# A fused softmax maximum: the pass that adds bias or mask writes the negated, scaled row maximum

## The chip, the cores and the metric

The kernel runs on one core of a Trainium2 chip. The metric is the device time of one launch in microseconds (us), the median over runs of the kernel. Engines are named PE (TensorE, matmuls; PEld its weight loads), DVE (VectorE), ACT (ScalarE), POOL (GpSimd) and SP (SyncE, which issues the DMAs).

## The reference, cut to what matters

The program is a transformer stack on 512 tokens of width 1024 in fp32: four layers of a first block (MLA, sliding-window attention with sinks, attention with a forget gate ("fox"), MLA again), then a second block with four mixers, two of them attentions, a feed-forward part and a gated addition. Every attention is a softmax over rows of scores:

```python
s = einsum(q, k) * scale                      # MLA, fox, second block
s = s + c_q[:, None] - cum_t[None, :]         # fox only: forget gate
s = where(k_pos <= q_pos, s, -1e30)           # causal mask, or a window in the sliding-window layer
p = softmax(s, axis=-1)
o = einsum(p, v)
# the sliding-window layer has a sink per head:
m = maximum(max(s, axis=-1), sink)
p = exp(s - m)
p = p / (sum(p, axis=-1) + exp(sink - m))
```

A number that is constant along a row of `s` (such as `c_q`) changes no softmax.

## The kernel before, in words

There are 72 heads in all: 16 in each of the four layers of the first block and 8 in the second block. Each head goes once through `attend` (L395 to L461). A head has 512 queries, which are four blocks of 128 (i = 0 to 3, one query on each partition). In the causal attentions block i has 128, 256, 384 or 512 keys, in the sliding-window layer 128, 256, 256 and 256.

For a head, in program order: PE writes the score products of a block to PSUM (tiles ps_s; L159 to L161 in the MLA layers, L240 and L241 elsewhere). DVE reads them once (L408, in the trace CUSTOM_DVE_ANT_0 with a DVE_READ_ACCUMULATOR2_ANT behind it): it adds the bias or mask, writes the sum to the tile p in SBUF and leaves the maximum of each row in a column of the small tile st (128 x 4 for the four blocks). Small instructions on st then make the bias of the exponential: one on DVE for the MLA and second-block heads (L417), two for fox (L414 and L415, which add and take away the row's own forget value `cq`), two for the sliding window (L419 and L420, which also take in the sink) and there one more on ACT (L421, the sink's own exponential). ACT takes the exponential of the four blocks in place (L424) and leaves their row sums in st. DVE inverts these (L427) and multiplies p by them (L432). PE transposes p in pieces of 128 x 128 (L448), ACT and DVE split the transposed tile into a high and a low part (L186, pth; L187, ptl), PE multiplies by the values (L457, tile ps_o), and ACT and DVE add the two halves up (L467, L468). In the second block a step of a top-k search on DVE (`tick`, L930 and L931) stands between the row maxima and the small instructions.

Beside a head, PE has the projections of the next pair of heads and gates. Their weights come by DMA, ACT rounds them to a high part (L140), and POOL takes the low part (L141).

The order on each engine is not the program order. The tile framework is opened with `schedule_with_timeline_sim=True`: it places the instructions of all engines by a simulation of their times, within the data dependences, so an instruction that is taken away can move others on every engine. Each engine then works its own list in order.

Of the kernel before, what the change touches and what calls it, by code (L numbers as in the profile page):

```python
# [11 lines left out]
AF = mybir.ActivationFunctionType  # L12
ALU = mybir.AluOpType
PSUM = bass.MemoryType.PSUM

P, S, D, T = 128, 512, 1024, 4
# [74 lines left out]
class Kern:  # L91
# [300 lines left out]
        return nxt  # L392


    def attend(s, s_mm, k0s, bias, scale, v, sink=None, shift=None):  # L395


        nc = s.nc
        w = [(i + 1 - k0s[i]) * P for i in range(T)]
        off = [sum(w[:i]) for i in range(T)]  # L400
        sc = s.t("p", [P, sum(w)])
        st = s.t("st", [P, 8, T])
        for grp in (([[3], [2, 0], [1]] if w[3] == 512 else [[0, 2], [1, 3]])):
            ps = s.p("s")
            c = 0
            for i in grp:
                s_mm(ps[:, c:c + w[i]], i, k0s[i])
                nc.vector.tensor_tensor_reduce(out=sc[:, off[i]:off[i] + w[i]], in0=ps[:, c:c + w[i]], in1=bias(i),  # L408
                                               op0=ALU.add, op1=ALU.max, scale=1.0, scalar=-3e38,
                                               accum_out=st[:, 0, i:i + 1])  # L410
                c += w[i]
        s.tick(4)
        if shift is not None:
            nc.vector.scalar_tensor_tensor(st[:, 0], st[:, 0], scale, shift, op0=ALU.mult, op1=ALU.add)  # L414
            nc.vector.tensor_sub(st[:, 1], shift, st[:, 0])  # L415
        elif sink is None:
            nc.vector.tensor_scalar_mul(st[:, 1], st[:, 0], -scale)  # L417
        else:
            nc.vector.tensor_scalar(st[:, 0], st[:, 0], scale, sink, op0=ALU.mult, op1=ALU.max)  # L419
            nc.vector.tensor_scalar_mul(st[:, 1], st[:, 0], -1.0)  # L420
            nc.scalar.activation(st[:, 4], st[:, 0], AF.Exp, bias=sink, scale=-1.0)  # L421
        for i in range(T):
            a = sc[:, off[i]:off[i] + w[i]]
            nc.scalar.activation(a, a, AF.Exp, bias=st[:, 1, i:i + 1], scale=scale, accum_out=st[:, 2, i:i + 1])  # L424
        if sink is not None:
            nc.vector.tensor_add(st[:, 2], st[:, 2], st[:, 4])
        nc.vector.reciprocal(st[:, 3], st[:, 2])  # L427
        for i in range(T):
            a = sc[:, off[i]:off[i] + w[i]]
            how = ("vvvv" if "cq" in s.phase_tags else "aavp")[i]  # L430
            if how == "v":
                nc.vector.tensor_scalar_mul(a, a, st[:, 3, i:i + 1])  # L432
            elif how == "a":
                nc.scalar.mul(a, a, st[:, 3, i:i + 1])
            else:
                nc.gpsimd.tensor_mul(a, a, st[:, 3, i:i + 1].to_broadcast([P, w[i]]))
        s.tick(2)
        o = s.p("o")
        first = True
        for grp in (([[0], [1, 3], [2]] if w[3] == 512 else [[0, 1], [2, 3]])):  # L440
            ps = s.p("t")
            n, js = 0, []
            for j in grp:
                qs = [i for i in range(j, T) if k0s[i] <= j]
                js.append((j, n, len(qs) * P))
                for i in qs:
                    c = off[i] + (j - k0s[i]) * P
                    nc.tensor.transpose(ps[:, n:n + P], sc[:, c:c + P], s.ident)  # L448
                    n += P
            ph = s.t("pth", [P, S], R)  # L450
            pl = s.t("ptl", [P, S], R)
            s.split(ps[:, :n], ph[:, :n], pl[:, :n])
            s.tick(2)
            for j, c, m in js:
                vj = v(j)
                for k, pp in enumerate((ph, pl)):
                    s.last_mm = nc.tensor.matmul(o[:, j * P:j * P + m], vj, pp[:, c:c + m], start=first,  # L457
                                                 stop=k == 1 and grp[-1] == max(2, grp[-1]) and j == grp[-1],
                                                 skip_group_check=True)
                    first = False  # L460
        return o  # L461
# [189 lines left out]
    def swa(s, j, li, xT, g_next):  # L651
        nc, I = s.nc, s.I
        Win, Wo = I["swa_w_in"][j], I["swa_w_out"][j]
        sinks = s.bcast_row(I["swa_sinks"][j], "gq", 32)
        vt = [s.t(g, [P, T, 2, 2, 64], R, name="v") for g in ("ckv", "cq")]
        s.v_proj(Win, 1280, 256, xT, lambda t, ps: s.v_split(ps, [v[:, t] for v in vt]))
        oT = s.act(8)
# [18 lines left out]
        def head(d, p, e):  # L676
# [1 line left out]
            q, (kd, kl), win = d  # L678
            return s.attend(lambda out, i, k0: s.qk_mm(out, i, k0, q, e, kd, kl), [0, 0, 1, 2],
                            lambda i: win[:, e, 128:] if i == 0 else win[:, e], 0.125, s.vsel(vt[p // 4], (p % 4) // 2),  # L680
                            sink=sinks[:, hd:hd + 1])

        s.pairs(range(8), prep, head, Win, 1536, xT, oT)
        return s.layer_end(Wo, oT, li, g_next)
# [2 lines left out]
    def fox(s, j, li, xT, g_next):  # L687
# [61 lines left out]
        def head(d, p, e):  # L749
            q, (k, kl), v, bs = d  # L750
            return s.attend(lambda out, i, k0: s.qk_mm(out, i, k0, q, e, k[:, e], kl[:, e]), [0] * T,
                            lambda i: bs[e][i], 0.125, s.vsel(v, e), shift=cq[:, :, 2 * p + e])

        s.pairs([6, 7, 0, 1, 2, 3, 4, 5], prep, head, Win, 3088, xT, oT)
        return s.layer_end(Wo, oT, li, g_next)
# [386 lines left out]
```

## Time and profile before

| | |
|---|---|
| median of 3 runs | 1753.9 us (1746.76 to 1757.82) |
| the profiled execution | 1751.54 us, of it 1749.8 us span in the trace |
| PE | busy 1679.9 us, 96% of the span, 8818 matmuls |
| DVE, ACT, POOL | busy 954.7, 873.0, 853.3 us |
| mean granted TensorE clock | 0.983 of 2.4 GHz |
| the six stages in order | MLA to about 298 us, sliding window to 472, fox to 775, MLA to 1033, mixers to 1285, feed-forward and the rest to 1750 |

A row of a view by stage gives how long each engine was busy in a stretch and the clock that TensorE was granted there, as a share of 2.4 GHz (0.50 is 1.2 GHz). A waits row says who stood still, whose result released it, for how long in total, how often, and the longest time.

### The profile page before, as it was taken

Reading aid. Unit: us, or ns where it says so; the run is one execution under the profiler, and the core shown is the slowest. Engines: PE = TensorE matmul, PEld = TensorE weight load, DVE = VectorE, ACT = ScalarE, POOL = GpSimd, SP = SyncE. Lnnn points to the kernel's source line nnn. Section 1 sums busy time; section 2 is a strip of 40 time slices with the busy share of each in tenths; the row PEclk is TensorE's granted clock in tenths of the full one; section 3 lists DMA queues with packets and bytes.
Section 4 is the critical chain, followed back from the end, with each engine's and each line's share of the span. In section 5 each row is a group of like instructions: output and inputs, shape, how many; then the busy total and the mean of one; then the engine's idle time right before and its main releaser. Section 6 shows DMA issues by size and latency. Waiting matters only on the chain.

```text
span 1749.8 us, 25693 instructions
## 1 busy us (share of the span) xinstructions
PE 1679.9 (96%) x8818; PEld 1430.5 (82%) x8818; DVE 954.7 (55%) x2223; ACT 873.0 (50%) x2054; POOL 853.3 (49%) x775
## 2 busy tenths in 40 slices
PE   7999999999899999999999998999999999999999
PEld 7888878887788888878888878878788888888877
DVE  4587654668663565666487665599544222210063
ACT  4576544666445665643576643755554333332251
POOL 1644544434255665625644524745644444443571
PEclk9999999999899999999999999999999999999999
DMA  5444534322023323414444523332323333322331
GB/s 170 130 101 115 166 105 139 91 67 85 26 74 97 108 79 87 124 60 130 115 114 103 180 62 75 91 85 67 109 76 103 98 97 97 97 97 78 106 100 73
DMA packets 190339, 173.91 MB, mean 99 GB/s; under 512 B 14280, under 2 KB 154952, under 8 KB 190208
## 3 DMA queue, kind: packets, MB, share of 16 engines
q1 hardware_dynamic: 190208, 172.27, 34.2%
q8 instruction: 70, 1.15, 0.3%
q14 instruction: 61, 0.50, 0.1%
HBM read 150.94 MB, written 6.87 MB: 90 GB/s over the span
## 4 chain that ended last, share of the span: by engine, by line
PE 54%; DVE 7%; issue 2%; ACT 2%; POOL 2%; DMA 1%; SPq 0%; ACTq 0%; POOLq 0%; DVEq 0%
PE ps_acc L159 11%; PE ps_acc L160 11%; PE ps_acc L161 11%; PE ps_s L160 4%; PE ps_s L159 4%; PE ps_s L161 4%; PE ps_o L457 2%; PE ps_t L448 2%; DVE p L432 1%; ACT p L424 1%; POOL wl L141 1%; DVE p L408 1%; DVE ptl L187 1%; DVE sel L931 1%; DVE m L930 1%
## 5 line engine op out<-in xcount | busy, mean ns | idle before, releaser
L141 POOL TENSOR_TENSOR wl<-wr,wh 128x512 fp32r<-128x512 f32 (+2 forms) x362 | 473.0, 1317 | 423.7 <-ACT wh L140 413.1
L140 ACT CAST wh<-wr 128x512 fp32r<-128x512 f32 (+2 forms) x368 | 223.3, 613 | 372.9 <-PE ps_acc L160 140.2
L159 PE MATMUL ps_acc<-act,wh 128*128 128x512 f32 (+1 forms) x880 | 332.4, 378 | 0.3 <-ACT act L186 0.2
L160 PE MATMUL ps_acc<-act,wh 128*128 128x512 f32 (+1 forms) x880 | 331.0, 376 | 0.3 <-DVE act L187 0.2
L161 PE MATMUL ps_acc<-act,wl 128*128 128x512 f32 (+1 forms) x880 | 331.0, 376 | 0.0
L160 PEld LDWEIGHTS ps_acc<-act,wh 128*128 128x128 f32 x880 | 166.1, 189 | 27.3 <-DVE act L187 0.7
L159 PEld LDWEIGHTS ps_acc<-act,wh 128*128 128x128 f32 x880 | 166.2, 189 | 27.2 <-ACT act L186 0.8
L161 PEld LDWEIGHTS ps_acc<-act,wl 128*128 128x128 f32 x880 | 165.6, 188 | 27.7
L424 ACT ACTIVATE p<-p,st 128x256 f32<-128x256 f32 (+3 forms) x288 | 153.5, 537 | 34.8 <-DVE st L415 18.4
L432 DVE TENSOR_SCALAR p<-p,st 128x256 f32<-128x256 f32 (+3 forms) x264 | 134.1, 566 | 1.8
L159 PE MATMUL ps_acc<-wh,act 128*128 128x256 f32 (+3 forms) x384 | 131.7, 343 | 3.0 <-DVE v L625 1.3
L187 DVE TENSOR_TENSOR ptl<-ps_t,pth 128x512 fp32r<-128x512 f32 (+1 forms) x200 | 117.4, 596 | 29.9 <-ACT pth L186 28.9
L448 PE MATMUL ps_t<-c_ident,p 128*128 128x128 f32 x672 | 117.2, 284 | 13.9 <-DVE p L432 12.0
L186 ACT CAST pth<-ps_t 128x512 fp32r<-128x512 f32 (+1 forms) x200 | 100.0, 516 | 59.3 <-PE ps_t L448 54.4
L160 PE MATMUL ps_acc<-wl,act 128*128 128x256 f32 (+3 forms) x384 | 127.8, 333 | 0.0
L161 PE MATMUL ps_acc<-wh,act 128*128 128x256 f32 (+3 forms) x384 | 127.6, 334 | 0.2 <-DVE act L187 0.2
L448 PEld LDWEIGHTS ps_t<-c_ident,p 128*128 128x128 f32 x672 | 82.6, 144 | 30.4 <-DVE p L432 14.9
L457 PE MATMUL ps_o<-ptl,v 128*128 128x256 f32 (+3 forms) x288 | 89.4, 339 | 8.0 <-DVE ptl L187 7.8
L457 PE MATMUL ps_o<-pth,v 128*128 128x256 f32 (+3 forms) x288 | 90.6, 320 | 6.4 <-DVE og L468 4.2
L159 PEld LDWEIGHTS ps_acc<-wh,act 128*128 128x128 f32 x384 | 75.5, 197 | 11.0 <-DVE v L625 1.5
L160 PEld LDWEIGHTS ps_acc<-wl,act 128*128 128x128 f32 x384 | 75.4, 196 | 5.2 <-issue 0.5
L161 PEld LDWEIGHTS ps_acc<-wh,act 128*128 128x128 f32 x384 | 74.5, 195 | 5.5 <-DVE act L187 0.7
(371 smaller groups left out, 3785.5 us busy)
## 6 DMA issues: line engine op xcount, KB each, us to landing
wr<-in_w_gate_up_dram SPq DMA_DIRECT2D x88, 256.0 KB, 2.8
wr<-in_fox_w_in_dram SPq DMA_DIRECT2D x60, 256.0 KB, 3.0
wr<-in_w_in_dram SPq DMA_DIRECT2D x48, 256.0 KB, 2.9
wr<-in_w_down_dram SPq DMA_DIRECT2D x44, 256.0 KB, 2.6
wr<-in_swa_w_in_dram SPq DMA_DIRECT2D x40, 256.0 KB, 2.9
wr<-in_mla_w_in_dram SPq DMA_DIRECT2D x32, 256.0 KB, 3.1
qk<-qk SPq DMA_DIRECT2D x32, 256.0 KB, 3.2
wr<-in_mla_w_out_dram SPq DMA_DIRECT2D x32, 256.0 KB, 3.4
```

The source lines that it names most:

```text
L140: nc.scalar.copy(h, raw)
L141: (nc.vector if dve else nc.gpsimd).tensor_sub(l, raw, h.bitcast(F32))
L159: mm(out, lh, rh, start=first, stop=False)
L160: mm(out, lh, rl, start=False, stop=False)
L161: return mm(out, ll, rh, start=False, stop=last)
L186: s.nc.scalar.copy(hi, src)
L187: s.nc.vector.tensor_sub(lo, src, hi.bitcast(F32))
L408: nc.vector.tensor_tensor_reduce(out=sc[:, off[i]:off[i] + w[i]], in0=ps[:, c:c + w[i]], in1=bias(i), op0=ALU.add, op1=ALU.max, scale=1.0, ...
L424: nc.scalar.activation(a, a, AF.Exp, bias=st[:, 1, i:i + 1], scale=scale, accum_out=st[:, 2, i:i + 1])
L432: nc.vector.tensor_scalar_mul(a, a, st[:, 3, i:i + 1])
L448: nc.tensor.transpose(ps[:, n:n + P], sc[:, c:c + P], s.ident)
L457: s.last_mm = nc.tensor.matmul(o[:, j * P:j * P + m], vj, pp[:, c:c + m], start=first, stop=k == 1 and grp[-1] == max(2, grp[-1]) and j == ...
```

## The change

The pass L408 now takes the minimum instead of the maximum, of the sum times `-scale`, so that p holds the negated scaled scores and st the negated row maximum in units of the exponent. The start value of the minimum is 3e38 or, in the sliding-window layer, a column of a new small tile `tops` with the negated sinks, made once in that layer's program by one ACT instruction. The exponential takes p with scale -1.0 and st as it stands. The DVE instructions L414, L415, L417, L419 and L420 are gone, 104 in all; ACT has one more. Fox's heads no longer read the row's own forget value.

```diff
-    def attend(s, s_mm, k0s, bias, scale, v, sink=None, shift=None):
+    def attend(s, s_mm, k0s, bias, scale, v, sink=None, top=None):
...
                 nc.vector.tensor_tensor_reduce(out=sc[:, off[i]:off[i] + w[i]], in0=ps[:, c:c + w[i]], in1=bias(i),
-                                               op0=ALU.add, op1=ALU.max, scale=1.0, scalar=-3e38,
-                                               accum_out=st[:, 0, i:i + 1])
+                                               op0=ALU.add, op1=ALU.min, scale=-scale,
+                                               scalar=3e38 if top is None else top, accum_out=st[:, 0, i:i + 1])
                 c += w[i]
         s.tick(4)
-        if shift is not None:
-            nc.vector.scalar_tensor_tensor(st[:, 0], st[:, 0], scale, shift, op0=ALU.mult, op1=ALU.add)
-            nc.vector.tensor_sub(st[:, 1], shift, st[:, 0])
-        elif sink is None:
-            nc.vector.tensor_scalar_mul(st[:, 1], st[:, 0], -scale)
-        else:
-            nc.vector.tensor_scalar(st[:, 0], st[:, 0], scale, sink, op0=ALU.mult, op1=ALU.max)
-            nc.vector.tensor_scalar_mul(st[:, 1], st[:, 0], -1.0)
-            nc.scalar.activation(st[:, 4], st[:, 0], AF.Exp, bias=sink, scale=-1.0)
+        if sink is not None:
+            nc.scalar.activation(st[:, 4], st[:, 0], AF.Exp, bias=sink)
         for i in range(T):
             a = sc[:, off[i]:off[i] + w[i]]
-            nc.scalar.activation(a, a, AF.Exp, bias=st[:, 1, i:i + 1], scale=scale, accum_out=st[:, 2, i:i + 1])
+            nc.scalar.activation(a, a, AF.Exp, bias=st[:, 0, i:i + 1], scale=-1.0, accum_out=st[:, 2, i:i + 1])
...
         sinks = s.bcast_row(I["swa_sinks"][j], "gq", 32)
+        tops = s.t("cqt", [P, 64], name="tops")[:, :sinks.shape[-1]]
+        nc.scalar.mul(tops, sinks, -1.0)
...
-                            sink=sinks[:, hd:hd + 1])
+                            sink=sinks[:, hd:hd + 1], top=tops[:, hd:hd + 1])
...
-                            lambda i: bs[e][i], 0.125, s.vsel(v, e), shift=cq[:, :, 2 * p + e])
+                            lambda i: bs[e][i], 0.125, s.vsel(v, e))
```

What this moves is seen in the order of each engine's list. The lists below print what an instruction writes and reads with its tile numbers, and in brackets which engine's semaphore it waits for; ISA is the pass L408 (L409 in the changed file) or, with st alone, its read of the accumulator. First DVE in the sliding-window layer, from the last pass of that layer's fourth head (p_3671, st_3672) on, before the change:

```order
L408 ISA p_3671,st_3672<-ps_s_3680,win_3406 128x256 [waits PE_49]
L408 ISA st_3672 128x1
L230 TENSOR_TENSOR qk_4013<-ps_acc_3975,qk_4012 64x512 [waits Activation_49]
L468 TENSOR_TENSOR og_3405<-ps_o_3537,og_3405 64x512 [waits Activation_49]
L419 TENSOR_SCALAR st_3672<-st_3672,gq_3077 128x4 [waits DVE_49]
L408 ISA p_3817,st_3818<-ps_s_3819,win_3569 128x128 [waits DMAHW1_49,PE_49]
L408 ISA st_3818 128x1
L187 TENSOR_TENSOR ptl_3650<-ps_t_3644,pth_3649 128x512 [waits Activation_49]
L408 ISA p_3817,st_3818<-ps_s_3826,win_3569 128x256 [waits PE_49]
L408 ISA st_3818 128x1
L187 TENSOR_TENSOR ptl_3662<-ps_t_3657,pth_3661 128x384 [waits Activation_49]
L420 TENSOR_SCALAR st_3672<-st_3672 128x4 [waits DVE_49]
```

Between the last accumulator read of st_3672 and the second small instruction on it stand nine instructions, among them two passes of the next head. The same head on DVE after the change (p_3651, st_3652):

```order
L409 ISA p_3651,st_3652<-ps_s_3653,win_3392,tops_3063 128x128 [waits PE_49]
L409 ISA st_3652 128x1
L462 TENSOR_TENSOR og_3391<-ps_o_3519,og_3391 64x512 [waits Activation_49]
L409 ISA p_3651,st_3652<-ps_s_3660,win_3392,tops_3063 128x256 [waits PE_49]
L409 ISA st_3652 128x1
L187 TENSOR_TENSOR ptl_3630<-ps_t_3624,pth_3629 128x512 [waits Activation_49]
L409 ISA p_3651,st_3652<-ps_s_3653,win_3392,tops_3063 128x256 [waits PE_49]
L409 ISA st_3652 128x1
L409 ISA p_3651,st_3652<-ps_s_3660,win_3392,tops_3063 128x256 [waits PE_49]
L409 ISA st_3652 128x1
L187 TENSOR_TENSOR ptl_3642<-ps_t_3637,pth_3641 128x384 [waits Activation_49]
```

Its four passes stand there with two other instructions between them, and no small instruction on st follows. Now ACT at the same head, before:

```order
L421 ACTIVATE st_3672<-st_3672,gq_3077 128x4 [waits DVE_49]
L474 CAST act_3221<-og_3405 128x512 [waits Pool_49]
L424 ACTIVATE p_3671,st_3672<-p_3671,st_3672 128x128 [waits DVE_49]
L424 ACTIVATE p_3671,st_3672<-p_3671,st_3672 128x256 x3
```

The four exponentials stand together behind one wait (the row with x3 is three of them). After the change (L418 is the exponential, L415 the sink's):

```order
L418 ACTIVATE p_3651,st_3652<-p_3651,st_3652 128x128 [waits DVE_49]
L418 ACTIVATE p_3651,st_3652<-p_3651,st_3652 128x256 [waits DVE_49]
L186 CAST pth_3629<-ps_t_3624 128x512 [waits PE_49,Activation_49]
L468 CAST act_3207<-og_3391 128x512 [waits Pool_49]
L186 CAST pth_3641<-ps_t_3637 128x384 [waits PE_49,Activation_49]
L140 CAST wh_4219<-wr_4217 128x512 [waits DMAHW7_49,PE_49]
L228 CAST qk_3986<-ps_acc_3949 64x512 [waits PE_49]
L229 CAST qk_3986<-ps_acc_3949 64x512
L418 ACTIVATE p_3651,st_3652<-p_3651,st_3652 128x256 [waits DVE_49]
L415 ACTIVATE st_3652<-st_3652,gq_3061 128x4 [waits DVE_49]
L418 ACTIVATE p_3651,st_3652<-p_3651,st_3652 128x256
```

The first two exponentials stand ahead of the splits and casts of other heads and of weights, each with a wait of its own on DVE, and the third one and the sink's wait again. Last, ACT's list at the start of the program after the change (tops is the new instruction, L650):

```order
L186 CAST act_72<-ps_t_126 128x4x128 [waits PE_49]
L140 CAST qk_169<-wr_170 128x288 [waits DMAHW4_49]
L140 CAST qk_174<-wr_175 128x288 [waits DMAHW5_49]
L650 ACTIVATE tops_3063<-gq_3061 128x16 [waits DMAHW7_49]
L186 CAST act_73<-ps_t_133 128x4x128 [waits PE_49]
```

The scheduler has put the sliding-window layer's new instruction into the first rows of the program, behind a wait for the DMA of the sinks and ahead of the last split of the transposed input (act_73).

## Rows read from the trace of the kernel before

**Rows 1.** The page's first lines: span, and busy time of each engine with its share and its instructions.
```profile
span 1749.8 us, 25693 instructions
PE 1679.9 (96%) x8818; PEld 1430.5 (82%) x8818; DVE 954.7 (55%) x2223; ACT 873.0 (50%) x2054; POOL 853.3 (49%) x775
```

**Rows 2.** Busy time by stretch, for the five stretches with attention heads (MLA, sliding window, fox, MLA, mixers with heads) and their sum: start and end, length, then busy us and instructions of PE, PEld, DVE, ACT, POOL, the granted clock, DMA share and GB/s.
```profile
78.00:298.00 220.00, 213.19 (x1188) 181.93 (x1187) 149.13 (x382) 127.37 (x323) 98.91 (x87) 0.99 0.45 126
318.00:472.00 154.00, 141.25 (x714) 117.67 (x713) 113.19 (x317) 94.47 (x255) 58.59 (x45) 0.91 0.23 67
553.00:775.00 222.00, 214.68 (x1194) 183.98 (x1193) 143.11 (x365) 137.24 (x330) 124.58 (x125) 0.99 0.32 92
880.00:1033.00 153.00, 148.00 (x810) 125.81 (x809) 115.28 (x309) 102.64 (x273) 69.03 (x63) 0.99 0.44 124
1156.00:1285.00 129.00, 119.01 (x596) 98.16 (x595) 102.30 (x258) 73.04 (x171) 71.37 (x61) 0.95 0.31 88
sum 878.00, PE 836.13 PEld 707.55 DVE 622.99 ACT 534.75 POOL 422.48; mean PE 167.23 PEld 141.51 DVE 124.60 ACT 106.95 POOL 84.50
```

**Rows 3.** Who PE waited for, over the whole span: us in total, times, longest us.
```profile
PE ps_t L448 <- DVE p L432: 12.0, 17, 1.7
PE ps_o L457 <- DVE ptl L187: 7.8, 11, 2.7
...
PE ps_s L240 <- DVE st L408: 6.2, 10, 1.6
...
PE ps_o L457 <- DVE og L468: 4.2, 8, 1.0
...
PE ps_o L457 <- ACT pth L186: 2.0, 4, 0.8
```

**Rows 4.** The removed instructions as groups of the whole span: count, then busy us and mean ns of one, and idle time of DVE just before them.
```profile
L417 DVE TENSOR_SCALAR st<-st 128x4 f32<-128x4 f32 x40 | 17.3, 433 | 0.5
...
L414 DVE SCALAR_TENSOR_TENSOR st<-st,cqt 128x4 f32<-128x4 f32 x16 | 7.6, 477 | 0.3
L415 DVE TENSOR_TENSOR st<-cqt,st 128x4 f32<-128x4 f32 x16 | 6.3, 394 | 0.3
L419 DVE TENSOR_SCALAR st<-st,gq 128x4 f32<-128x4 f32 x16 | 6.2, 389 | 0.3
L420 DVE TENSOR_SCALAR st<-st 128x4 f32<-128x4 f32 x16 | 5.2, 323 | 0.3
```

**Rows 5.** DVE in order of time at the fourth head of the sliding window: start us, us, instruction. The first row is the accumulator read of the head's last pass.
```profile
345.66 0.08 DVE L408 DVE_READ_ACCUMULATOR2_ANT st<- 128x1 f32 x1
...
347.08 0.23 DVE L419 TENSOR_SCALAR st<-st,gq 128x4 f32<-128x4 f32 x1
...
348.84 0.16 DVE L420 TENSOR_SCALAR st<-st 128x4 f32<-128x4 f32 x1
```

**Rows 6.** ACT in order of time at the same head: the sink's exponential, a cast of other work, the first of the four exponentials.
```profile
348.07 0.30 ACT L421 ACTIVATE st<-st,gq 128x4 f32<-128x4 f32 x1
348.47 0.62 ACT L474 CAST act<-og 128x512 fp32r<-128x512 f32 x1
349.03 0.40 ACT L424 ACTIVATE p<-p,st 128x128 f32<-128x128 f32 x1
```

**Rows 7.** Busy time by stretch, as in rows 2, for the 9 us around that head.
```profile
343.00:347.00 4.00, 2.17 (x13) 1.33 (x11) 3.97 (x10) 3.26 (x8) 1.27 (x1) 0.98 0.29 77
347.00:352.00 5.00, 4.81 (x18) 4.33 (x19) 4.72 (x21) 4.86 (x14) 2.60 (x2) 0.50 0.16 47
```

**Rows 8.** The exponentials and the passes as groups over the whole span, and who ACT waited for at the exponentials (us in total, times, longest us).
```profile
L424 ACT ACTIVATE p<-p,st 128x256 f32<-128x256 f32 (+3 forms) x288 | 153.5, 537 | 34.8 <-DVE st L415 18.4 <-DVE st L417 12.0 <-DVE st L420 4.2
...
L408 DVE CUSTOM_DVE_ANT_0 p<-ps_s,win 128x128 f32<-128x128 f32 (+1 forms) x64 | 23.7, 385 | 17.9 <-PE ps_s L241 16.2 <-PE ps_t L448 1.3
```

**Rows 9.** Durations of DVE instructions with one operand in PSUM and one in SBUF: name, count, then ns least, median and most, first and last start. L384 has a scalar by pointer (a column of st in SBUF) beside them, L324 an immediate one; the third is the sliding window's pass.
```profile
L384 DVE SCALAR_TENSOR_TENSOR f<-ps_s,st,sel x6: 740/742/744, 1297.9 to 1691.9; 128x512 f32<-128x512 f32 x6
L324 DVE SCALAR_TENSOR_TENSOR x<-x,ps_acc x17: 668/680/689, 251.6 to 1059.8; 128x512 f32<-128x512 f32 x17
L408 DVE CUSTOM_DVE_ANT_0 p<-ps_s,win x64: 271/414/425, 311.1 to 457.4; 128x256 f32<-128x256 f32 x48, 128x128 f32<-128x128 f32 x16
```

**Rows 10.** One of the small instructions, the POOL instruction beside it, and the least, median and most ns of the small instruction.
```profile
318.29 1.29 DVE L420 TENSOR_SCALAR st<-st 128x4 f32<-128x4 f32 x1
318.27 1.29 POOL L141 TENSOR_TENSOR wl<-wr,wh 128x512 fp32r<-128x512 f32 x1 [1.92 <-ACT wh L140]
L420 DVE TENSOR_SCALAR st<-st x16: 152/170/1295, 318.3 to 459.1; 128x4 f32<-128x4 f32 x16
```

**Rows 11.** The start of the program: SP's issue of the sinks, the time of such a DMA from issue to landing (least, median, most us), and ACT's last split of the transposed input.
```profile
11.58 0.33 SPq L258 DMA_DIRECT2D gq<-in_swa_sinks_dram  x1
DMA to landing us min/median/max: 3.0/3.0/3.0
14.61 0.59 ACT L186 CAST act<-ps_t 128x512 fp32r<-128x512 f32 x1
```

## The prediction

> **What bounds the kernel now.** I read the page's busy times first. PE is busy 1679.9 of 1749.8 us, and the change leaves its 8818 matmuls alone [rows 1]. So nothing that the change removes is on PE, and it can only win back time in which PE stands still or runs slowly. Next I read busy time by stretch, for the five stretches in which attention heads run [rows 2]. There PE is busy 836.1 of 878.0 us, which leaves 41.9 us idle. The reader is to see that the sliding window stands out: 12.8 us idle in 154, DVE busy for 113.2 (73%), and a granted clock of 0.91. Third, the waits of PE [rows 3]: 12.0 us for the normalised p of a head (L432, the end of the softmax chain), 7.8 for the low part of the transposed p, 6.2 for a pass to free its score bank, 4.2 for the addition of the output halves. All four are DVE results. Only 2.0 us are ACT's directly.
>
> The order of time at one head shows how such a wait comes about. The last pass leaves its maximum at 345.74 (345.66 and 0.08), the first small instruction starts at 347.08, the second at 348.84 [rows 5], and the first exponential at 349.03 [rows 6]: 3.3 us from the last maximum to the first exponential, for two instructions of 0.23 and 0.16 us. The rest is other work that the scheduler has put between them on DVE. Around this head PE is busy for 2.17 of 4 us, and in the 5 us that follow its granted clock is 0.50, the 1.2 GHz level [rows 7]. An idle time of PE is therefore paid a second time, in slower matmuls: the sliding window at 0.91 loses 0.09 of 154 us, 13.9 us, and the mixers at 0.95 lose 0.05 of 129, 6.5 us, together 20.4 [rows 2].
>
> **The change part by part.** *DVE work.* Five groups go: 17.3, 7.6, 6.3, 6.2 and 5.2 us, together 42.6 us in 104 instructions [rows 4]. They are dear for 128 x 4 numbers. L420 has a median of 170 ns and a most of 1295, and in the long case it began 0.02 us behind a POOL subtraction and both took 1.29 us [rows 10]. So the sum goes by the groups' means, which hold such stalls, and not by the medians. In the sliding window the pass gains a pointer operand in SBUF. The trace has no such pass; its nearest rows are two DVE instructions that read 512 columns of PSUM and one SBUF tensor, at 742 ns with a pointer scalar and 680 without [rows 9]. I take the difference, 62 ns, for 64 passes: 4.0 us, with 0 and 62 ns as the ends. The other 224 passes only change immediates and the kind of comparison: nothing, and at most the same 62 ns, 13.9 us of DVE. Net, DVE loses 38.6 us, 6% of its 623.0 in these stretches [rows 2].
>
> *The chain of a head.* The exponential of a block now waits for its own pass alone, and the order shows ACT taking the first two ahead of other casts while the last two passes are still to come. What stood behind the last maximum, 3.3 us to the first exponential and then all four exponentials at about half a us [rows 6, 8], becomes the exponential of the last block (in the sliding window behind the sink's, 0.30 us). The longest of PE's 17 waits for p is 1.7 us, half of what this head's chain loses [rows 3]. In an unchanged order all 12.0 us would go; at the other end is nothing, because the scheduler builds its order from the shorter chain and can draw the transposes nearer by as much. I take two thirds, 8 us, as the chain loses about twice the longest wait.
>
> *Other waits for DVE.* These are 7.8, 6.2 and 4.2 us, 18.2 in all [rows 3]. Their low end is 6% of them, 1.1 us, if they shrink as DVE's work does; their high end is all 18.2. I take 2, near the low end, since these waits hang on where DVE's list puts an instruction and not on its sum. What is late next there is the reciprocal and the four multiplications on DVE, which the change leaves alone.
>
> *The clock.* 10 of the 41.9 us idle are to go, a quarter; a quarter of 20.4 is 5. I take 4 (ends 0 and 20.4), because where the idle time goes and where the clock is low need not be the same places.
>
> *What is added.* ACT's new instruction stands near the start of its list, behind the DMA of the sinks and ahead of the last split of the input. That DMA is issued at 11.58 and lands 3.0 us later, at 14.58; the split began at 14.61 [rows 11]. So ACT is held by the instruction itself, 0.30 us as the sink's exponential [rows 6]; a landing 1 us later would cost 1 us, as PE has little else to do there. I take +0.3. The issue on SP's queue stands where it stood. Fox's heads lose a dependence on `cq`, which was ready long before: nothing.
>
> *Sum.* -8 - 2 - 4 + 0.3 = -13.7 us, so 1751.5 becomes 1737.8 in the terms of the profiled execution. The median of the three runs lies 2.4 us above that execution: 1740.
>
> **The rivals.** *The order gives it all back* (1753). PE's list is made anew around the shorter chain, and DVE's load falls by only 6%. If the transposes come nearer by as much as the chain shrinks, only the low end of the second term is left, 1.1 us. For it: the scheduler kept PE at 95% in these stretches with the longer chain too. Against it: fewer instructions and fewer waits bind it.
>
> *The clock comes back* (1723). If the idle times in the sliding window fall below what lets the clock drop, its second price goes with them: 12.0, half of 18.2 and half of 20.4, 31.3 us. For it: the low clock follows the idle time directly [rows 7]. Against it: DVE was busy 3.97 of the 4 us before, and the removed instructions are only a tenth of its 113.2 us there (6.2 and 5.2) [rows 2, 4, 7].
>
> *ACT's list stands still* (1780, slower). A head's exponentials used to wait once, behind work that was done; now up to four instructions of a head wait for DVE, and what stands behind them on ACT (splits of other heads, casts of the weights, shown in the order) waits too. ACT stood still 34.8 us before exponentials, 0.48 us per head [rows 8]. Three more such waits per head are 1.45 us, 104 us over 72 heads. ACT has 343 idle us in these stretches (878.0 less 534.8) [rows 2], so ACT itself does not become the bound; it turns slower by over 1% when more than a sixth of the 104 us reaches PE with no gain beside it. At a quarter it is 26 us: 1780. Against it: PE waited for ACT's splits for 2.0 us only [rows 3].
>
> *The pass is held by POOL* (1754). With the pointer to `tops` the sliding window's pass reads two operands from SBUF beside PSUM. If that lets a running POOL instruction hold it, 64 passes meet one with POOL's share there, 58.6 of 154 us, and lose half of 1.29 us each: 15.8 us of DVE against the 11.4 that left that layer [rows 2, 4, 10]. The layer's gain is gone and some 4 us lost, which about cancels what the other layers win. Against it: L384 reads PSUM, an SBUF tensor and a pointer in SBUF, and its six took 740 to 744 ns, so none was held [rows 9]. The Trainium skill ("SBUF — State Buffer", Who interferes with whom) says that a DVE instruction with at most one SBUF input outside the two-port modes does not contend with GpSimd, and that one with two SBUF inputs contends with a GpSimd instruction that reads SBUF. By that rule the change could take the pass from the first kind to the second, if a pointer scalar counts as an input, which the page does not say; the even times of L384 speak for no. The same section has a one-source DVE instruction in a two-port mode blocked for a whole GpSimd instruction, and L420's 1.29 us agree.
>
> *The change doesn't do what it says.* The order shows the separate waits and the 104 instructions gone, so I give this nothing of its own.
>
> **How the numbers follow.** Forecast near 1740 (1728 to 1752): 0.46. Order gives it back: 0.25. Clock comes back: 0.17. ACT stands still: 0.08. Pass held: 0.04. A difference of 1%, 17.5 us, is about what a measurement of this kernel can tell from none. Below 1736.4 lie the clock case and 0.18 of the forecast's 0.46: faster 0.35. Above 1771.4 lies the ACT case: slower 0.08. The rest, 0.57, is within 1%. The range goes from 1722 to 1757: it takes in the forecast, the giving back and the held pass, and the near half of the clock case.
>
> **What would show it.** Right: PE's waits for p fall from 12.0 us to about 4; DVE's busy time falls by nearly 40 us; the first exponential of a head starts before its last pass has ended; the sliding window's granted clock rises above 0.91 and its stretch is shorter by 5 to 8 us. The pass with a pointer shows its own price: about 60 ns more than 414, without a long tail. Wrong: ACT's idle time before exponentials well over 34.8 us together with PE waits for pth or for weights (ACT's list); the same 12 us of waits for p in other places (order); single passes of over 1 us in the sliding window (POOL). A gain in the stretch after the heads, where there is no softmax, would mean that the cause is another.

## The result, and the profile after

The changed kernel takes 1729.4 us (median of 4 runs, 1726.22 to 1731.57), the kernel before 1755.2 in the same comparison. The ratio over the runs is 0.9871 (95% interval 0.9845 to 0.9897). In a second comparison (changed_again, below) it was 0.9875 (0.9855 to 0.9894). The forecast was 1740 and its range 1722 to 1757, so the time is inside the range and 10.6 us below the forecast. The profiled executions are 23.8 us apart (1751.54 and 1727.79), and what follows divides these 23.8. One run of e6 below took 4074.3 us, more than twice any other run, and counts in no ratio.

First the page's top lines after the change, which answer to [rows 1]:

```profile
span 1726.0 us, 25630 instructions
PE 1666.1 (97%) x8818; PEld 1420.5 (82%) x8818; DVE 935.4 (54%) x2119; ACT 878.7 (51%) x2055; POOL 855.1 (50%) x775
```

PE has the same 8818 matmuls and is busy 13.8 us less for them, so over half of the gain is not idle time but faster matmuls. Its idle time in the span falls by the other 10.0 us (1749.8 less 1679.9 is 69.9, 1726.0 less 1666.1 is 59.9). DVE lost its 104 instructions but only 19.3 us, half of the forecast's 38.6.

To see where the 23.8 us went, the span is cut at each stretch's first and last pass (L408 before, L409 after), which gives MLA, sliding window, fox, MLA, mixers. Busy time by stretch with the columns of [rows 2], before:

```profile
74.78:225.90 151.12, 146.33 (x809) 125.18 (x808) 114.92 (x322) 98.77 (x269) 67.33 (x63) 0.99 0.47 125
311.08:457.74 146.66, 133.91 (x684) 111.46 (x683) 109.17 (x313) 90.95 (x242) 57.30 (x44) 0.92 0.24 72
550.10:755.97 205.87, 200.25 (x1132) 173.20 (x1131) 131.35 (x341) 128.45 (x310) 119.95 (x122) 0.99 0.34 98
868.69:1014.81 146.12, 141.89 (x791) 121.74 (x789) 112.71 (x316) 98.88 (x269) 67.06 (x62) 0.99 0.47 129
1144.93:1269.92 124.99, 115.97 (x574) 95.85 (x573) 103.88 (x276) 66.98 (x159) 69.33 (x60) 0.95 0.30 85
```

And after:

```profile
73.32:222.74 149.42, 142.84 (x792) 121.93 (x791) 108.42 (x303) 101.90 (x274) 67.36 (x63) 0.99 0.48 126
311.44:441.00 129.56, 125.53 (x681) 107.11 (x681) 96.40 (x276) 90.27 (x243) 54.10 (x42) 0.96 0.27 80
533.61:739.29 205.68, 200.41 (x1135) 172.37 (x1134) 129.97 (x312) 131.25 (x313) 120.54 (x121) 1.00 0.35 98
850.03:994.33 144.30, 140.42 (x791) 120.11 (x789) 108.09 (x303) 101.26 (x273) 66.97 (x62) 1.00 0.49 131
1124.90:1245.94 121.04, 113.20 (x575) 93.67 (x574) 103.98 (x269) 68.80 (x163) 68.61 (x60) 0.97 0.32 92
```

The sliding window alone is 17.1 us shorter (146.66 to 129.56). PE's idle time there falls from 12.75 to 4.03 us, 8.7 us, and its busy time by 8.4 us for 684 and 681 recorded matmuls, at a granted clock of 0.96 instead of 0.92. The other four stretches give 1.7, 0.2, 1.8 and 4.0 us. The stretch between the first MLA and the sliding window grew by 3.5 us (225.90 to 311.08 before, 222.74 to 311.44 after), so that 13.6 of the 17.1 us are left when this way is counted in. After the last pass of all nothing changed (479.9 and 480.1 us to the end of the span).

Who PE waited for after the change, over the whole span (us in total, times, longest us):

```profile
PE ps_o L451 <- DVE ptl L187: 7.0, 8, 2.6
PE ps_o L451 <- DVE og L462: 6.8, 9, 1.4
PE ps_s L240 <- DVE st L409: 4.1, 11, 0.6
...
PE ps_t L442 <- DVE p L426: 3.5, 4, 1.4
...
PE ps_o L451 <- ACT pth L186: 1.6, 5, 0.6
```

Against [rows 3], the wait for the normalised p fell from 12.0 to 3.5 us and is no longer the first. The three other waits for DVE were 18.2 and are 17.9.

How a head now runs is seen at the fourth head of the sliding window again, the one of [rows 5, 6]. ACT's exponentials and DVE's last pass, picked from the order of time (start us, us, instruction):

```profile
340.50 0.40 ACT L418 ACTIVATE p<-p,st 128x128 f32<-128x128 f32 x1
...
341.45 0.51 ACT L418 ACTIVATE p<-p,st 128x256 f32<-128x256 f32 x1 [0.47 <-DVE st L409]
...
344.75 0.48 DVE L409 CUSTOM_DVE_ANT_0 p<-ps_s,win,tops 128x256 f32<-128x256 f32 x1
345.15 0.08 DVE L409 DVE_READ_ACCUMULATOR2_ANT st<- 128x1 f32 x1
...
346.21 0.51 ACT L418 ACTIVATE p<-p,st 128x256 f32<-128x256 f32 x1
...
346.72 0.28 ACT L415 ACTIVATE st<-st,gq 128x4 f32<-128x4 f32 x1
346.91 0.49 ACT L418 ACTIVATE p<-p,st 128x256 f32<-128x256 f32 x1
```

Two exponentials are done before the last pass is read at 345.23 (345.15 and 0.08), and the last ends at 347.40, 2.2 us behind it. Before the change the first exponential alone began 3.3 us behind. The same quantity for all heads, the time from the end of a head's last maximum read to the end of its last exponential, is called its chain below. It is worked out by matching the engines' lists to the trace, and given as a mean over the heads of a layer: in the sliding window it fell from 4.2 to 1.45 us, in the other layers it was 3.6 to 4.7 and is 1.1 to 1.6.

The groups that answer to [rows 8], and the multiplications (busy us and mean ns, then idle us before them and what ended it):

```profile
L418 ACT ACTIVATE p<-p,st 128x256 f32<-128x256 f32 (+3 forms) x288 | 155.7, 542 | 75.3 <-DVE st L409 74.4
...
L426 DVE TENSOR_SCALAR p<-p,st 128x256 f32<-128x256 f32 (+3 forms) x264 | 142.8, 597 | 1.7
...
L409 DVE CUSTOM_DVE_ANT_0 p<-ps_s,win,tops 128x128 f32<-128x128 f32 (+1 forms) x64 | 27.4, 444 | 5.6 <-PE ps_s L241 5.0 <-PE ps_t L442 0.2
```

The pass of the sliding window by its durations (least, median and most ns), as in [rows 9]:

```profile
L409 DVE CUSTOM_DVE_ANT_0 p<-ps_s,win,tops x64: 335/476/485, 311.4 to 440.6; 128x256 f32<-128x256 f32 x48, 128x128 f32<-128x128 f32 x16
```

ACT stood still 75.3 us before exponentials, twice the 34.8 of before. The pass with the pointer has a median of 476 ns, 62 above [rows 9], and a longest of 485: none of the 64 was held.

### The profile page after: what moved, and what is told of

Read it like the earlier page. It is cut to its first block, busy times and chain, and to the rows that moved or that the text cites. A ratio compares the mean times of both kernels' runs of the same rounds, so it can differ in the third digit from the quotient of the medians.

```text
span 1726.0 us, 25630 instructions
## 1 busy us (share of the span) xinstructions
PE 1666.1 (97%) x8818; PEld 1420.5 (82%) x8818; DVE 935.4 (54%) x2119; ACT 878.7 (51%) x2055; POOL 855.1 (50%) x775
## 4 chain that ended last, share of the span: by engine, by line
PE 80%; DVE 10%; issue 3%; DMA 3%; ACT 2%; POOL 2%; SPq 0%; POOLq 0%; DVEq 0%; ACTq 0%
PE ps_acc L159 17%; PE ps_acc L160 17%; PE ps_acc L161 16%; PE ps_s L159 5%; PE ps_s L160 5%; PE ps_s L161 5%; PE ps_o L451 4%; PE ps_t L442 3%; DVE p L426 1%; DVE sel L927 1%; DVE p L409 1%; PE ps_t L250 1%; DVE m L926 1%; DVE ptl L187 1%; DMA qk<-qk 1%
## 5 line engine op out<-in xcount | busy, mean ns | idle before, releaser
L418 ACT ACTIVATE p<-p,st 128x256 f32<-128x256 f32 (+3 forms) x288 | 155.7, 542 | 75.3 <-DVE st L409 74.4
L161 PEld LDWEIGHTS ps_acc<-act,wl 128*128 128x128 f32 x880 | 165.7, 188 | 26.9
L426 DVE TENSOR_SCALAR p<-p,st 128x256 f32<-128x256 f32 (+3 forms) x264 | 142.8, 597 | 1.7
L159 PE MATMUL ps_acc<-wh,act 128*128 128x256 f32 (+3 forms) x384 | 129.3, 337 | 3.3 <-DVE v L619 1.3
L442 PE MATMUL ps_t<-c_ident,p 128*128 128x128 f32 x672 | 110.1, 279 | 5.4 <-DVE p L426 3.5
L442 PEld LDWEIGHTS ps_t<-c_ident,p 128*128 128x128 f32 x672 | 80.1, 142 | 18.2 <-DVE p L426 4.5
L409 DVE CUSTOM_DVE_ANT_0 p<-ps_s,c_mask 128x256 f32<-128x256 f32 (+3 forms) x128 | 59.9, 482 | 38.4 <-PE ps_s L161 23.9
```

The lines of the kernel that those rows point to most:

```text
L159: mm(out, lh, rh, start=first, stop=False)
L161: return mm(out, ll, rh, start=False, stop=last)
L418: nc.scalar.activation(a, a, AF.Exp, bias=st[:, 0, i:i + 1], scale=-1.0, accum_out=st[:, 2, i:i + 1])
```

## The experiments

The expectations name theories by letter. C: the chain of a head is shorter, so PE idles less and keeps its clock, mainly in the sliding window. D: DVE has 104 instructions less to do, and its free time is the gain. O: the scheduler came upon a better order, whatever the arithmetic. E, in the last two: the chain costs as good as nothing, and what a copy on ACT costs is ACT's time, wherever the head is. Ratios are to the kernel before in the same comparison; the last column is the length from the read of the first pass's maximum in the sliding window to the end of the read of the last, some 0.3 us less than with the first pass itself. These two columns come from one profiled run each, and runs of one kernel spread over 10 us and more: the profiled runs of e1 and e3 are the longest of their six, those of e2 and e4 the shortest of theirs.

| run | median us | ratio (95% interval) | chain there, us | window, us |
|---|---|---|---|---|
| before | 1755.2 | 1 | 4.20 | 146.5 |
| after | 1729.4 | 0.9871 (0.9845 to 0.9897) | 1.45 | 129.4 |
| changed_again | 1732.2 | 0.9875 (0.9855 to 0.9894) | 1.45 | 129.5 |
| e1_window_only | 1739.4 | 0.9903 (0.9883 to 0.9922) | 1.40 | 129.3 |
| e2_rest_only | 1745.0 | 0.9949 (0.9931 to 0.9967) | 4.17 | 144.4 |
| e6_before_order | 1755.5 | 1.0013 (0.9994 to 1.0031) | 4.17 | 143.5 |
| e4_idle_steps | 1733.8 | 0.9881 (0.9862 to 0.9899) | 1.25 | 129.8 |
| e7_gate_dve | 1744.9 | 0.9954 (0.9937 to 0.9970) | 3.64 | 138.4 |
| e3_gate_act | 1736.5 | 0.9899 (0.9880 to 0.9918) | 3.13 | 136.8 |
| e8_gate_window | 1733.6 | 0.9885 (0.9867 to 0.9904) | 3.09 | 133.7 |
| e9_gate_rest | 1732.6 | 0.9876 (0.9855 to 0.9898) | 1.41 | 128.7 |
| e5_sink_late | 1723.3 | 0.9840 (0.9817 to 0.9862) | 0.90 | 129.7 |

**The change repeated** (changed_again), the changed kernel without an edit, as a second reference.

> The changed kernel as it is, beside the next three on one chip: 1729 (1725 to 1734) by every theory; it is the yardstick for them.

It gave 0.9875, the same within the intervals.

**In which layers the gain lies** (e1_window_only, e2_rest_only). In the first, only the heads with a sink take the new lines, and all others the old ones; the second is the reverse.

```diff
+                if sink is not None:      # e2: if sink is None
                     ... op0=ALU.add, op1=ALU.min, scale=-scale, ...
+                else:
+                    ... op0=ALU.add, op1=ALU.max, scale=1.0, scalar=-3e38, ...
```

> The change in the sliding-window layer alone; MLA, fox and the second block keep the maximum and their small steps. Theory C (the chain from a head's last maximum to its last exponential is shorter, 4.2 us before and 1.4 after; what PE then no longer waits for, and the clock that it keeps, is the gain; the sliding window has least other PE work to cover the chain): 16.9 of the 23.8 us between the two traces lie in that layer's stretch, so 1738 (1733 to 1743). Theory D (the gain is DVE time): this layer gives up 11.4 us of small steps and takes on 4.0, 7 of 38.6 us, a fifth of the gain: 1750. Theory O (any new order of the scheduler moves the time by this much, whatever was removed): no relation to the layer, anything from 1730 to 1755, and a stretch of the sliding window that is not shorter.

> The change everywhere but in the sliding-window layer, which keeps its maximum and its two small DVE steps. C: the other 7 of 24 us, 1748 (1743 to 1752), and with the kernel that has the change in the sliding window alone the gains add up to the whole. D: four fifths of the gain, 1734. O: no relation.

The sliding window alone gives 0.9903 and the 56 other heads 0.9949. Their product is 0.9852, inside the first interval of the whole change and just outside the second, so within the noise the two parts add up: about two thirds from 16 of 72 heads. Each shortened the chain only where it was applied (in e1 the others stay at 3.6 to 4.6 us, in e2 they are at 1.1 to 1.6).

**Whether it is only another order** (e6_before_order). The kernel before, with its four exponentials written in another order.

```diff
-        for i in range(T):
+        for i in (3, 2, 0, 1):
```

> The kernel before, with nothing but the program order of a head's four exponentials changed (3, 2, 0, 1 in place of 0, 1, 2, 3), which gives the scheduler another order to start from and leaves work and dependences as they were. C and D: 1754 (1748 to 1760). O: the order alone moves the time by 10 us or more either way.

The time did not move (1.0013, interval across 1), although the sliding window became 3.0 us shorter: its first pass came later, the way to it from the first MLA grew by 5.8 us, and fox, the second MLA and the mixers are each about 1 us longer. In this one trial, order by itself shifts single stretches by a few us and leaves the total; it is not the source of 23.8. In e2, which has the new lines in all other layers and so another order, the window also stays at 144.4.

**DVE's time or the chain** (e4_idle_steps, e7_gate_dve). These two part C from D. The first puts DVE's 104 small steps back, but nobody reads what they write. The second puts back 72, one a head, and the exponentials and the sink's wait for it.

```diff
+        nc.vector.tensor_scalar_mul(st[:, 5], st[:, 0], -scale)      # e4, behind the exponentials
+        if ...:      # sliding window and fox: a second one
+            nc.vector.tensor_scalar_mul(st[:, 6], st[:, 0], -1.0)
```
```diff
+        nc.vector.tensor_copy(st[:, 1], st[:, 0])      # e7, ahead of them
...
-            ... AF.Exp, bias=st[:, 0, i:i + 1], scale=-1.0, ...
+            ... AF.Exp, bias=st[:, 1, i:i + 1], scale=-1.0, ...
```

> The changed kernel with the removed DVE work put back beside the chain: after a head's passes DVE computes as many 128 x 4 steps as before (one, or two in the sliding window and fox), whose results nobody reads; 104 DVE instructions more, nothing waits for them. C: the exponentials start as early as in the change, so nearly all of the gain stays: 1732 (1728 to 1738). D: DVE is as loaded as before: about 1753. O: no forecast.

> The changed kernel, but the bias of the four exponentials is a copy of the four columns that DVE makes (72 instructions of 128 x 4, some 0.2 to 0.4 us each): one small step on DVE between the last maximum and the exponentials, as the MLA layers had it before, now in every layer; sink and forget value stay folded away. C: the step waits in DVE's list behind other work again, 1.7 us as in the MLA layers before, and the four exponentials follow it: 1744 (1737 to 1750), slower than with ACT's copy (1736.5). D: DVE gets back some 25 of the 38.6 us, on the chain or not: 1745. With the idle steps at 1733.8 already on record, D is held only if this kernel is no slower than that one.

The dead steps cost next to nothing, 0.9881 against 0.9875. Fewer steps, for which the exponentials wait, lose nearly two thirds of the gain, 0.9954. Busy times from the pages of the two, e4 first:

```profile
PE 1667.5 (96%) x8818; PEld 1422.7 (82%) x8818; DVE 964.7 (56%) x2223; ACT 877.5 (51%) x2055; POOL 852.2 (49%) x775
```
```profile
PE 1678.6 (96%) x8818; PEld 1430.7 (82%) x8818; DVE 949.0 (54%) x2191; ACT 873.4 (50%) x2055; POOL 852.3 (49%) x775
```

The sliding window's row of busy time by stretch, e4 and e7:

```profile
307.32:437.36 130.04, 124.65 (x682) 105.99 (x682) 102.39 (x309) 91.27 (x245) 54.80 (x43) 0.97 0.27 80
```
```profile
313.75:452.44 138.69, 128.63 (x679) 108.09 (x679) 101.06 (x291) 87.96 (x237) 54.67 (x42) 0.95 0.25 75
```

And the first of PE's waits in that layer, e4 and e7:

```profile
PE ps_s L240 <- DVE st L409: 2.8, 5, 0.9
```
```profile
PE ps_s L240 <- DVE st L409: 4.6, 8, 1.3
PE ps_o L452 <- DVE og L463: 2.6, 3, 1.4
```

The four waits for DVE over the whole span, e4 and e7:

```profile
PE ps_o L454 <- DVE ptl L187: 6.8, 11, 2.4
PE ps_t L445 <- DVE p L429: 6.8, 9, 1.4
...
PE ps_s L240 <- DVE st L409: 4.8, 11, 0.9
...
PE ps_o L454 <- DVE og L465: 3.2, 6, 0.8
```
```profile
PE ps_t L443 <- DVE p L427: 8.8, 11, 2.4
...
PE ps_s L240 <- DVE st L409: 6.3, 13, 1.3
PE ps_o L452 <- DVE ptl L187: 6.1, 11, 2.7
PE ps_o L452 <- DVE og L463: 5.7, 11, 1.4
```

In e4 DVE is busier than in any other kernel here, the one before included (964.7 against 954.7 us), and the gain stays. In e7 it is busy 15.7 us less than in e4, and the ratio is 0.0073 worse, 13 us. In the sliding window DVE has about the same load (102.4 and 101.1 us), but PE is idle 10.1 us instead of 5.4 and busy 4.0 longer for the same matmuls. D falls; a step's price is its place in the chain. In that layer what came back is not the wait for p by name (0.4 us in e4, 0.2 in e7): with the order made anew around the longer chain, PE waits for a score bank and for the addition of the halves. Over the span the wait for p is 8.8 us in e7, but 6.8 in e4 too, against 3.5 in the changed kernel; the four together are 26.9 us in e7 and 21.6 in e4, against 21.4.

**What the early start of single blocks is worth** (e3_gate_act, e8_gate_window, e9_gate_rest). A copy of the maxima on ACT makes the exponentials wait for the whole head again, but not in DVE's list: in all heads, in the sliding window's, in all others.

```diff
+        nc.scalar.copy(st[:, 1], st[:, 0])      # e8: if sink is not None; e9: if sink is None
...
-            ... AF.Exp, bias=st[:, 0, i:i + 1], scale=-1.0, ...
+            ... AF.Exp, bias=st[:, 1, i:i + 1], scale=-1.0, ...
```

> The changed kernel, but the four exponentials of a head take their bias from a copy that ACT makes of all four columns (72 ACT instructions of some 0.3 us more), so that none can start before the head's last pass; no step comes back to DVE. C: the chain from the last maximum to the last exponential is 0.3 and about 2.2 us again, some 2.6 in place of 1.4 (4.2 before): about half the gain, 1742 (1735 to 1748). D: DVE has as little to do as in the change: 1729 to 1731. O: no forecast.

> The changed kernel with ACT's copy ahead of the four exponentials in the sliding-window layer alone (16 ACT instructions more). Theory C, with the lengths of the sliding window's passes from first to last on record (146.7 us before, 136.6 with ACT's copy in all layers, 129.6 changed): this layer's stretch is near 136.6 again and the whole 1737 (1733 to 1741). Rival E (the chain is as good as free everywhere, and what ACT's copies cost is ACT's time: 72 instructions of some 0.3 us and the waits behind them): 16 of 72 copies, a quarter of the loss of 5 to 8 us: 1733.

> The changed kernel with ACT's copy ahead of the four exponentials everywhere but in the sliding window (56 ACT instructions more). C: the chain of MLA, fox and second-block heads is 3.4 us again in place of 1.5, but PE has other work there and lost 1 to 3 us a layer by it before: 1734 (1730 to 1739), and the sliding window's stretch stays near 129.6. E: three quarters of the loss: 1736.

In all heads the copy costs 0.0024 of the ratio against changed_again, some 4 us, which the intervals do not tell apart from nothing; C had expected about half of the gain to go, 1742 us. Yet it brings the chain back to 3.1 us in the window and the window to 136.8 us. Against the copy on DVE (e7) the intervals stand apart (0.9880 to 0.9918 and 0.9937 to 0.9970). So most of the gain comes from leaving DVE's list, and the early start of single blocks is the smaller part.

The two halves, 0.9885 and 0.9876, can't be told from the whole change by their intervals. By the profiles the window did react to its own gate (133.7 us, where C said about 136.6) and not to the others' (128.7), as C says; the total of e8 was nearer to E's. The windows of e3 and e8 have nearly the same chain, the same 677 recorded matmuls and nearly the same idle time of PE (8.2 and 8.7 us), but a clock of 0.95 and 0.99 and 128.9 and 125.2 us of busy time: the 3 us between them are the clock's, in two single runs. In e9 the first MLA's stretch is the shortest of all runs, 146.2 us, with a chain of 3.43 us, and the second MLA's the longest, 150.5, with 3.55, so outside the sliding window the chain's length does not order the stretches.

**The sink's exponential last** (e5_sink_late). It is written behind the four others.

```diff
-        if sink is not None:
-            nc.scalar.activation(st[:, 4], st[:, 0], AF.Exp, bias=sink)
         for i in range(T):
...
         if sink is not None:
+            nc.scalar.activation(st[:, 4], st[:, 0], AF.Exp, bias=sink)
```

> The changed kernel with the sink's own exponential written behind the four of the head, so that in the sliding window the last block's exponential need not stand behind it on ACT (0.30 us). C: at most 16 times 0.30 us less on that layer's chain, and PE now waits 1.2 us for p there: 1728 (1724 to 1732), not to be told from the changed kernel. D: the same as changed. O: any order can be worth 10 us or more: outside 1724 to 1734.

It took 1723.3 us, ratio 0.9840 (0.9817 to 0.9862), just under the range of C and D, which expected no difference, and so by as little in the range that O claimed. It has the lowest median of all, but its interval overlaps that of changed_again, and one of its four runs took 1731.8 us. The chain in the window is 0.90 us, and the stretch is no shorter (129.7 us). It holds more work, though. From the first pass of the window to the end of its last read, and on to the first pass of fox, in the changed kernel and in e5:

```profile
311.44:441.09 129.65, 125.62 (x682) 107.18 (x682) 96.49 (x278) 90.36 (x244) 54.10 (x42) 0.96 0.27 80
441.09:533.61 92.52, 90.64 (x528) 79.60 (x527) 47.39 (x84) 39.02 (x77) 46.97 (x45) 1.00 0.28 76
```
```profile
310.80:440.77 129.97, 125.61 (x695) 106.07 (x695) 97.02 (x283) 93.31 (x248) 56.72 (x44) 1.00 0.28 81
440.77:529.72 88.95, 87.38 (x515) 77.10 (x514) 42.92 (x79) 36.68 (x71) 44.21 (x43) 1.00 0.28 77
```

Thirteen matmuls moved from the way to fox into the window, which did them in the same time at a clock of 1.00 instead of 0.96, and the two stretches together are 3.2 us shorter. Another 1.8 lie in the mixers, whose heads have no sink (118.7 us against 120.5); e8, without this edit, has the same 118.7 there, so these are another order's. Whether the 3.2 come from the shorter chain or from another order is open.

Read down the table, the sliding window follows its chain: 143.5 to 146.5 us at a chain of 4.2, 138.4 at 3.6, 133.7 to 136.8 at 3.1, 128.7 to 129.5 at 1.4, and no less below that (129.8 at 1.25 and 129.7 at 0.90). PE's idle time in the stretch goes the same way: 10.2 to 12.8 us at 4.2, 10.1 at 3.6, 8.2 and 8.7 at 3.1, 4.0 to 5.4 below. Counted from the end of the first MLA, which takes in the way to the first pass, it is 231.8 to 234.6 us at 4.2, 222.6 to 226.4 at 3.6 and 3.1, and 214.2 to 218.6 at 1.4 and below.

## Why the prediction was right, and where its sizes were off

*The chain of a head* was right in mechanism and nearly in size: forecast 8 of 12.0 us, measured 8.5. That e4 keeps the gain and e7 loses it shows the mechanism and not only the sum. That the size came so near is in part luck: e4, with as short a chain and nearly the same time, has 6.8 us of waits for p. The four waits for DVE together are firmer, 30.2 us before, 21.4 after, 21.6 in e4 and 26.9 in e7, and PE's idle time fell by 10.0 us where 8 and 2 were forecast. The head that the prediction reads was also one of the slower ones: 3.3 us to its first exponential and 5.2 to the end of its last, where the layer's means are 2.3 and 4.2.

*Other waits for DVE* were forecast at 2 and gave 0.3, near nothing by name. The wait for a score bank fell by 2.1 us and the one for the halves' addition grew by 2.6. The reason given, that these waits hang on places in DVE's list and not on its sum, fits e4.

*The clock* was the term that was mis-sized. I scaled the loss of 20.4 us by the share of idle time that was to go, a quarter, and took 4. In the sliding window alone PE's busy time fell by 8.4 us for the same matmuls, in the mixers by 2.8. The idle time removed was mostly where the clock was low: 8.7 of the window's 12.75 us went, two thirds, and the quarter was an average over five stretches with different limits. Two thirds of that layer's own 13.9 us would have been 9.3, near the 8.4 measured. The sliding window gave 17.1 us where I said 5 to 8. Over the span PE's busy time fell by 13.8 us where the clock was to give 4, and those 9.8 are nearly the whole difference between the forecast's 13.7 and the 23.8 us between the profiled executions. The measured time lies between the forecast and the rival *the clock comes back* (1723). The window's clock is 0.96 and not 1. Busy time by stretch shows the two places where nearly all of the rest is lost, 10 us each:

```profile
341.44:351.44 10.00, 8.09 (x47) 6.25 (x47) 7.21 (x27) 8.80 (x23) 4.29 (x4) 0.98 0.27 80
351.44:361.44 10.00, 10.00 (x50) 8.49 (x50) 6.37 (x22) 7.80 (x23) 1.83 (x2) 0.84 0.18 52
...
421.44:431.44 10.00, 8.12 (x52) 6.87 (x51) 8.17 (x28) 7.33 (x22) 3.28 (x3) 1.00 0.42 124
431.44:441.44 10.00, 9.77 (x45) 8.36 (x45) 9.80 (x34) 8.40 (x27) 2.10 (x3) 0.66 0.09 27
```

PE was busy for 8.09 and 8.12 of 10 us, and in the 10 us that follow its clock is 0.84 and 0.66: what [rows 7] showed, twice more. The sum of idle time alone does not settle the clock, as e3 and e8 show with 0.95 and 0.99 at nearly the same idle time. How much of the clock's part would come without the idle part no run here separates.

*DVE's work* was over-estimated, without effect on the sum. The five groups (42.6 us) are gone and the pointer costs 62 ns a pass as taken, but DVE is relieved of 19.3 us where 38.6 were forecast. The multiplications L426 rose from a mean of 566 to 597 ns (134.1 to 142.8 us for 264, rows in the last section), other rows grew by some 7 us, and durations on DVE overlap: their sum fell by 23.5 us, the busy time by 19.3.

*What is added* at the start: the new instruction ran at 15.19 for 0.22 us, and the split behind it began at 15.47 instead of 14.61 [rows 11]. Of this 0.86 us the new instruction made about 0.3, as forecast; the split ahead of it was already 0.59 late (14.05 for 13.46). It cost nothing that lasted, as the first pass of the program came at 73.32 instead of 74.78.

*The rivals.* *The order* did not give the gain back; e6, and the 3.5 us lost ahead of the sliding window, show its size, a few us. *ACT's list stands still* was right in its first half, ACT's idle time before exponentials doubled, by 40.5 us where 104 were foreseen, but PE's waits for ACT's splits went from 2.0 to 1.6 us: ACT's idle time is not on the path. *The pass is held by POOL* falls with 335 to 485 ns: 23 of the 64 passes overlapped a POOL instruction in the trace, and none was held. The Trainium skill ("SBUF — State Buffer", Who interferes with whom) has a DVE instruction with two SBUF inputs contend with a GpSimd instruction that reads SBUF; these times agree with it only if a pointer scalar is no such input, which the page does not say.

*Signs named beforehand.* Waits for p near 4, the first exponential ahead of the last pass's end, a clock above 0.91 and a pass 60 ns dearer without a long tail came as written; DVE's nearly 40 us and the window's 5 to 8 us did not.

Open: why the sliding window follows its chain so closely while MLA's stretches, with as many heads in about the same time, hardly do. In part they had less to give: before the change PE stood idle there for 4.8 and 4.2 us at a clock of 0.99, in the sliding window for 12.75 at 0.92. Open too are the 6 us of e5, if they are real.

## What to carry to other kernels

Price a small step by the time from its input's arrival to its reader's start, in the order of time, and not by its duration: here 0.39 us of work held the exponentials for 3.3 at one head and for 2.3 on the layer's mean. Look for idle time and low clock in the same stretch, and size the clock's return from that stretch alone. To tell whether a removed step paid by its time or by its place, put its work back where nobody waits for it, then where somebody does.

## What the runs showed of the hardware that was not expected

Taking 42.6 us of small steps off DVE shortened its busy time by 19.3. The multiplications of before as a group (L432), and their least, median and most ns:

```profile
L432 DVE TENSOR_SCALAR p<-p,st 128x256 f32<-128x256 f32 (+3 forms) x264 | 134.1, 566 | 1.8
```
```profile
L432 DVE TENSOR_SCALAR p<-p,st x264: 274/406/2899, 80.8 to 1273.0; 128x128 f32<-128x128 f32 x64, 128x384 f32<-128x384 f32 x52, 128x256 f32<-128x256 f32 x16
```

The same after:

```profile
L426 DVE TENSOR_SCALAR p<-p,st x264: 266/408/1571, 79.6 to 1250.2; 128x128 f32<-128x128 f32 x64, 128x384 f32<-128x384 f32 x52, 128x256 f32<-128x256 f32 x16
```

Their median stayed (406 and 408 ns) while their mean grew by 31. The single durations in the traces show two kinds with nothing between. A multiplication with no POOL instruction beside it takes at most 1.09 times the shortest of its shape. Every one that takes more than 1.3 times overlaps a POOL instruction, and of these there are 61 before, 75 after and 59 in e3. The removed steps were of the same two kinds: 40 of the 104 took over 300 ns, all of them beside POOL as in [rows 10], and without POOL none took more than 232. So the price of such instructions hangs on what runs beside them, and the order decides that: with as many DVE instructions as the changed kernel, e3 has DVE busy for 923.8 us instead of 935.4. That the 14 held multiplications more met the same POOL instructions that had held the removed steps is supposed, not shown.

The pointer to `tops` costs the pass about the same at both of its widths. Split by shape, its median rose from 286 to 348 ns at 128 columns and from 419 to 478 at 256.
